# Hymba layer on one core: the last norm's tiles copied out of their banks, three tiles a chain at the end, and the SSD's out-projection put ahead of the LRU's in the last part

## The chip, the core and the metric

The kernel runs on one core of a Trainium2 chip. The time is device microseconds of one launch. The kernel before has a median of 3129.86 us over three runs (3123.33 to 3131.66); its profiled execution took 3120.88 us.

In the text PE is TensorE's matmul, PEld its weight load, DVE is VectorE, ACT is ScalarE, POOL is GpSimd, and SP is SyncE, which issues almost all DMAs. "Banks" are the eight PSUM tiles of 128 x 512 fp32 that matmuls write to. All times are in microseconds from the start of the profiled span.

## What is computed

One layer of a hybrid decoder, in fp32, for 2048 prompt tokens and 32 sample tokens (8 sequences of 4), with a width of 1024 and a feed-forward width of 4096. Cut to what matters here:

```python
h = rmsnorm(x, g_mix)
proj = h @ w_in
# group A: conv, RG-LRU, gelu gate, group norm  -> y_lru (1024 columns)
# group B: conv, Mamba-2 SSD in chunks, silu gate, two group norms -> y_ssd (1024)
x = x + concatenate([y_lru, y_ssd], axis=-1) @ w_out
m = rmsnorm(x, g_mlp)
x = x + square(relu(m @ w_up)) @ w_down
y = rmsnorm(x, g_final)
```

Outputs are `y` for prompt and sample tokens, and the states that both groups carry on.

## The kernel before

**Layout and precision.** Activations lie transposed: 128 channels on the partitions, tokens along the row. An fp32 product is three fp32r matmuls of a high and a low half of each operand (`mm3`, lines 232 to 234). The halves of a weight come from `load_w`: a DMA into `raw` (line 217), an ACT copy to `wh` (219) and a DVE subtraction to `wl` (221).

**The mix phase** runs over three parts of 768, 672 and 640 tokens, each in two blocks of tokens (the last part: 384 and 256). A part is projected in, goes through eight pairs of SSD heads and eight LRU heads, and is projected out by `proj_add` (427 to 445). The SSD heads form two norm groups. The first group's out-projection runs in the middle of the heads, the second's at the end of the part beside the LRU's. For an output tile `o` of 128 channels and a block, `proj_add` lets PE fill a bank, and DVE multiplies it by the norm's row factors (444) and adds it to the residual `X2[o]` (445). For the second SSD group an output has 4 chunks of 128 inputs in 2 blocks, so 24 matmuls and two pairs of these DVE operations; one `load_w` serves two outputs. Line by line in the order of the program, at the end of each part:

- outputs 0 to 5 of the second SSD group; between them, by `hook`, the LRU's eight gated results are split into halves (488) and their norm is summed;
- all eight outputs of the LRU;
- outputs 6 and 7 of the second SSD group;
- squares of `X2` on ACT, added up on DVE (455), for the next norm: in the last part those of outputs 0 to 5 before the SSD's last two outputs, those of 6 and 7 after. `carried_out` writes the carried states out by way of `st` copies.

`residual_out` then closes the part by block: token sums by PE (466, bank `nx`), a reciprocal root on DVE (`rsqrt`, 246 to 252, ten small operations however many columns), its spreading to rows (294 and 296), eight multiplications (1296), and for each the stores to `mn_d` (1298) and `x2_d` (1299) in DRAM.

**Jobs.** Beside this, 64 jobs of six stages turn the MLP's weights into seven combined blocks in DRAM (`up_d`, `dn_d`): a load, four DVE additions, an ACT copy and two DVE subtractions (1133), two stores. `tick`, called from the heads and from `proj_add`, issues one stage whenever `clock[1]` has come up by one; a last `tick(999)` issues what is left.

**The MLP** runs over three blocks of columns (`MLP`: twice 348, 346 and 346). It multiplies 2 x 2 blocks of operands by seven products in place of eight. `front` loads the normed residual from `mn_d` (856), forms the seven operands and splits them into halves (834 on ACT, 835 on DVE). `up` (seven `product`s of 12 matmuls, 827) and `down` (four times seven) then alternate, eight times each pair. Weights come from DRAM into six buffers `mw` (818 for up, 956 for down). `down` loads the residual back into its `x2` tiles (963) in a column block's first round, and adds the products to it (946).

**The final norm** (`final`, 990 to 1025) of a column block is cut into six tiles of up to 128 tokens. A tile is a `step`: four transposes by PE into a bank for each of two halves of the channels (1006); ACT squares the bank into a buffer `yt` and sums along the row (1008); DVE adds the two sums (1011, 1012), takes the reciprocal root, and multiplies both banks by it and the gain into the same `yt` (1016); SP stores both (1022). There are three `yt` buffers. The steps of column blocks one and two are the `fill` of the next block: each is issued behind product 0, 2, 4 or 6 of the next block's first two `up`s (`FILL`), in two banks of a pool of their own (`fx`). The steps of the last block run at the very end, in the MLP's six banks.

**What sets the order.** A scheduler lays out each engine's instructions, with the order of the program as priority, and every engine runs its own in that order. SP too works in order: a DMA that waits for its data or its buffer holds up all those behind it. Pools give their buffers round robin, so an instruction waits until the buffer's last user is done.

Of the kernel before, what the change touches and what calls it, by code (L numbers as in the profile page):

```python
# [8 lines left out]
F32 = mybir.dt.float32  # L9
# [29 lines left out]
TP, TL, TO, TX = 0.9, 1.35, 1.0, 1.0  # L39

# [7 lines left out]
def hymba_step(ctx: ExitStack, tc: tile.TileContext,  # L48
# [754 lines left out]
    def mlp(residual):  # L803
# [5 lines left out]
        room["w"], room["nx"] = (tl, 6), psf  # L809
        def bank():  # L810
            return ps8.tile([128, 512], F32, tag="mb", name="mb")
# [4 lines left out]
        def weights(src, op, m):  # L816
            w = mp.tile([128, 2, 512], F32R, tag="mw", name="mw", bufs=6)
            nc.sync.dma_start(w[:, :, :m].bitcast(F32), src[:, op])
            return w
# [167 lines left out]
        def final(c0, n, x2, end=False):  # L987
# [11 lines left out]
            def step(o, m):  # L999
                ss = sf.tile([128, 8], F32, tag="ssq", name="ssq")  # L1000
                s2 = sf.tile([128, 2], F32, tag="s2", name="s2")
                yts, pss = [], []
                for hf in range(2):
                    ps = bank() if end else psf.tile([128, 512], F32, tag="nx", name="fx")
                    for k in range(4):
                        T.transpose(ps[:m, 128 * k:128 * k + 128], x2[4 * hf + k][:, o:o + m], ident)
                    yt = mq.tile([128, 512], F32, tag="yt", name="yt", bufs=3)
                    S.activation(yt[:m], ps[:m], AF.Square, accum_out=s2[:m, hf:hf + 1])  # L1008
                    yts.append(yt)
                    pss.append(ps)  # L1010
                V.tensor_add(ss[:m, 0:1], s2[:m, 0:1], s2[:m, 1:2])
                V.tensor_scalar(ss[:m, :1], ss[:m, :1], 1.0 / D, EPS, op0=ALU.mult, op1=ALU.add)
                rs = sf.tile([128, 8], F32, tag="rs", name="rs")
                rsqrt(rs[:m], ss[:m], 1, sf)
                for hf in range(2):
                    V.scalar_tensor_tensor(out=yts[hf][:m], in0=pss[hf][:m], scalar=rs[:m, 0:1],  # L1016
                                           in1=gfb[:m, 512 * hf:512 * hf + 512], op0=ALU.mult, op1=ALU.mult)

                    for a, e, ap, r in ((0, s0, y_p, 0), (s0, s1, y_s, -s0), (s1, NTOK, y_p, -NS)):
                        lo, hi = max(a, c0 + o), min(e, c0 + o + m)  # L1020
                        if lo < hi:
                            nc.sync.dma_start(dap(ap, (lo + r) * D + 512 * hf, [[D, hi - lo], [1, 512]]),
                                              yts[hf][lo - c0 - o:hi - c0 - o])

            return [lambda a=a: step(*a) for a in steps]

        mh, steps = front(*MLP[0])
# [80 lines left out]
    clock = [0, 0.0]  # L1108
# [38 lines left out]
    def tick(w):  # L1147

        n = len(stages)
        clock[1] += w  # L1150
        while clock[1] >= 1 and clock[0] < n * len(jobs):
            clock[1] -= 1
            j, st = divmod(clock[0], n)
            stages[st](j)
            clock[0] += 1
# [33 lines left out]
    for P in parts:  # L1189
        dt_front(P)  # L1190
# [86 lines left out]
        proj_add(P, w_out, 12, n1, bc1, range(6), {o: (lambda o=o: hook(o)) for o in range(6)})  # L1277
# [23 lines left out]
        proj_add(P, w_out, 0, nl, bcl, hooks={5: lambda: next(xn, None)})  # L1301
        next(xn, None)
        if P.last:
            carried_out(P)
            sums(range(6))
        proj_add(P, w_out, 12, n1, bc1, range(6, 8))
        for _ in xn:
            pass
        sums(range(6, 8) if P.last else range(8))
        if not P.last:  # L1310
# [42 lines left out]
```

## Time and profile before

| What | Value |
|---|---|
| Median of three runs | 3129.86 us (3123.33 to 3131.66) |
| The profiled execution | 3120.88 us, of which 3119.1 us are its span |
| TensorE's mean granted clock | 0.963 of full speed |
| Mix phase, to the last matmul of the out-projection | from 0 to 1692.7 us |
| First to last matmul of the MLP | from 1727.9 to 3080.3 us |
| From there to the end | 38.8 us |

In a row of a window table stand the stretch, its length, and for each engine its busy time and, in brackets, its instructions; then the clock that TensorE was granted (1.00 is full), the share of time in which the 16 DMA engines were busy, and what they moved. In a row of a timeline stand the start, the duration, the engine, the line, the operation, out<-in, the shape and the count of like instructions run together; in square brackets how long the engine had been idle ahead of it and whose signal it was put down to. SPq is SP's queue: the time for which it was at issuing DMAs.

### The profile page before, as it was taken

What the parts mean: (1) busy time and instruction counts of PE and PEld (TensorE: products, weight loads), DVE (VectorE), ACT (ScalarE), POOL (GpSimd) and SP (SyncE); (2) the same over time, 40 slices, a digit from 0 to 9 for tenths busy, and PEclk for the clock granted to TensorE, in tenths of its full rate; (3) what the DMA queues carried; (4) which work ended last, traced back from release to release, by engine and by line L of the source; (5) the groups of instructions that cost most, each with busy time, mean ns of one, the idle gap of its engine ahead of it and who ended that gap; (6) DMA issues with size and microseconds to landing.
All of it is one profiled execution on the core that took longest, in us unless ns stands there. A gap on an engine that the chain in (4) does not pass through costs nothing.

```text
span 3119.1 us, 49521 instructions
## 1 busy us (share of the span) xinstructions
PE 2896.6 (93%) x18150; PEld 2797.3 (90%) x18150; DVE 2183.2 (70%) x4463; ACT 1380.8 (44%) x2556; POOL 164.5 (5%) x270
## 2 busy tenths in 40 slices
PE   7999998999999897999987899999899999899996
PEld 6999897888989796998977899999799998899995
DVE  6888788788877878887896655557554547554546
ACT  5554785445348834535862332324332324323222
POOL 0000120010002200000210000000000000000000
PEclk9999998999999998999988899999999999999997
DMA  5555556766665677565666988888888888888884
GB/s 175 157 189 158 179 176 196 241 198 202 195 186 173 198 233 240 157 202 171 193 195 205 329 266 283 274 274 281 269 271 283 267 283 279 273 273 276 270 277 145
DMA packets 534482, 709.00 MB, mean 227 GB/s; under 512 B 44421, under 2 KB 414265, under 8 KB 534240
## 3 DMA queue, kind: packets, MB, share of 16 engines
q1 hardware_dynamic: 534016, 705.56, 71.0%
q8 instruction: 144, 2.36, 0.3%
q0 software_dynamic: 224, 0.27, 0.1%
q14 instruction: 98, 0.80, 0.1%
HBM read 541.43 MB, written 164.27 MB: 226 GB/s over the span
## 4 chain that ended last, share of the span: by engine, by line
PE 40%; DVE 4%; DMA 3%; ACT 1%; issue 1%; SPq 1%; DVEq 0%; ACTq 0%
PE mb L827 38%; DMA out_dram<-yt 1%; DMA mb<-mn_d 0%; DMA mw<-dn 0%; DMA dn<-jt 0%; DVE yt L1016 0%; SPq L1115 0%; PE mm L234 0%; PE mm L233 0%; PE mm L232 0%; DVE ahl L835 0%; ACT yt L1008 0%; ACT mhh L834 0%; DMA x<-x_d 0%; DVE jt L1133 0%
## 5 line engine op out<-in xcount | busy, mean ns | idle before, releaser
L232 PE MATMUL mm<-xh,wh 128*128 128x384 f32 (+3 forms) x2160 | 715.1, 332 | 32.7 <-ACT xe L398 14.2
L234 PE MATMUL mm<-xh,wl 128*128 128x384 f32 (+3 forms) x2160 | 706.5, 328 | 3.8 <-DVE wl L221 3.7
L233 PE MATMUL mm<-xl,wh 128*128 128x384 f32 (+3 forms) x2160 | 706.9, 328 | 0.1
L827 PE MATMUL mb<-ahh,mw 128*128 128x346 f32 (+1 forms) x2688 | 656.5, 324 | 20.8 <-DVE nt L249 8.7
L827 PE MATMUL mb<-mhh,mw 128*128 128x346 f32 (+1 forms) x2688 | 651.8, 322 | 19.3 <-ACT mhh L834 18.7
L827 PEld LDWEIGHTS mb<-ahh,mw 128*128 128x128 f32 x2688 | 473.0, 190 | 28.2 <-DVE nt L249 9.5
L827 PEld LDWEIGHTS mb<-mhh,mw 128*128 128x128 f32 x2688 | 474.9, 190 | 20.5 <-ACT mhh L834 19.6
L232 PEld LDWEIGHTS mm<-xh,wh 128*128 128x128 f32 (+1 forms) x2160 | 410.6, 190 | 49.8 <-ACT xe L398 17.5
L827 PE MATMUL mb<-mhl,mw 128*128 128x346 f32 (+1 forms) x1344 | 437.1, 325 | 0.0
L827 PE MATMUL mb<-ahl,mw 128*128 128x346 f32 (+1 forms) x1344 | 435.1, 324 | 0.3
L234 PEld LDWEIGHTS mm<-xh,wl 128*128 128x128 f32 (+1 forms) x2160 | 409.2, 190 | 12.5 <-DVE wl L221 6.0
L233 PEld LDWEIGHTS mm<-xl,wh 128*128 128x128 f32 (+1 forms) x2160 | 410.5, 190 | 3.9 <-issue 1.0
L946 DVE TENSOR_TENSOR x<-x,mb 128x346 f32<-128x346 f32 (+1 forms) x480 | 244.2, 514 | 147.2 <-PE mb L827 143.8
L219 ACT ACTIVATE wh<-raw 128x1024 fp32r<-128x1024 f32 (+1 forms) x159 | 165.5, 1042 | 254.6 <-PE mm L233 204.5
L827 PEld LDWEIGHTS mb<-ahl,mw 128*128 128x128 f32 x1344 | 255.0, 190 | 1.2 <-DVE ahl L835 1.0
L827 PEld LDWEIGHTS mb<-mhl,mw 128*128 128x128 f32 x1344 | 254.8, 190 | 0.0
L905 ACT ACTIVATE p<-mb 128x346 f32<-128x346 f32 (+1 forms) x48 | 21.9, 455 | 474.2 <-PE mb L827 474.2
L221 DVE TENSOR_TENSOR wl<-raw,wh 128x1024 fp32r<-128x1024 f32 (+1 forms) x159 | 190.9, 1201 | 21.5 <-ACT wh L219 18.9
L411 DVE SCALAR_TENSOR_TENSOR u<-xe,prm,u 128x768 f32<-128x768 f32 (+2 forms) x180 | 170.0, 945 | 17.6 <-ACT u L409 15.4
L232 PE MATMUL mm<-nh,wh 128*128 128x384 f32 (+2 forms) x384 | 130.8, 341 | 29.5 <-DVE x L445 26.5
L932 ACT ACTIVATE c<-c 128x346 f32<-128x346 f32 (+1 forms) x144 | 71.2, 494 | 192.8 <-DVE c L918 115.4
L1130 ACT ACTIVATE jh<-jt 128x1792 fp32r<-128x1792 f32 x64 | 108.6, 1697 | 105.2 <-DVE jt L1126 89.6
(303 smaller groups left out, 4240.7 us busy)
## 6 DMA issues: line engine op xcount, KB each, us to landing
mw<-up SPq DMA_DIRECT2D x336, 512.0 KB
mw<-dn SPq DMA_DIRECT2D x288, 512.0 KB
raw<-in_w_in_dram SPq DMA_DIRECT2D x108, 512.0 KB
up<-jh SPq DMA_DIRECT2D x32, 896.0 KB
up<-jt SPq DMA_DIRECT2D x32, 896.0 KB
dn<-jh SPq DMA_DIRECT2D x32, 896.0 KB
dn<-jt SPq DMA_DIRECT2D x32, 896.0 KB
raw<-in_w_out_dram SPq DMA_DIRECT2D x48, 512.0 KB
```

The lines of the kernel that those rows point to most:

```text
L219: S.activation(h, raw, AF.Copy)
L221: V.tensor_tensor(out=lo, in0=raw, in1=h.bitcast(F32), op=ALU.subtract)
L232: T.matmul(ps[:m, :n], h[:, k, :m], xh[:, c0:c0 + n], start=k == 0, stop=False)
L233: T.matmul(ps[:m, :n], h[:, k, :m], xl[:, c0:c0 + n], start=False, stop=False)
L234: T.matmul(ps[:m, :n], lo[:, k, :m], xh[:, c0:c0 + n], start=False, stop=k == nk - 1)
L411: V.scalar_tensor_tensor(out=u[:, :W], in0=xe[:, k:k + W], scalar=pc(wn, k * nt + j), in1=u[:, :W], op0=ALU.mult, op1=ALU.add)
L827: T.matmul(ps[:, :n], w[:, wi, c], x[:, :n], start=start and k == 0 and i == 0, stop=k == nk - 1 and i == 2, skip_group_check=not start)
L905: S.activation(p1[:, :n], x[:, :n], AF.Copy)
L932: S.activation(c[:, :n], c[:, :n], AF.Relu)
L946: V.tensor_tensor(out=c, in0=c, in1=ps[:, :n], op=op)
L1130: S.activation(h, jt[j], AF.Copy)
```

## The change

Four edits.

1. **The final norm.** `step` takes a list of tiles. Inside the MLP (`end` false) it is still one tile, but ACT now copies the bank into `yt` behind its square (line 1020 of the new kernel), and DVE multiplies `yt` in place of the bank, so the bank's last reader is the copy. At the end (`end` true) a step takes three tiles, with one reciprocal root of three columns, and DVE reads the banks as before. `yt` has six buffers in place of three.
2. **The order of the out-projection in the last part.** All eight outputs of the second SSD group come ahead of the LRU's. The squares of output `o - 1` are called for ahead of the LRU's output `o`, and those of output 7 at the end, behind `carried_out`.
3. **The first five up-weights** are requested (`ahead`) before `front` asks for its rows.
4. **The clock of the jobs** runs 5% faster in the last part (`TF`).

```diff
+TF = (1.0, 1.0, 1.05)
...
+        ahead = []
...
         def weights(src, op, m):
+            if src is up_d[0] and ahead:
+                return ahead.pop(0)
...
-            def step(o, m):
+            def step(tiles):
+                w = len(tiles)
                 ss = sf.tile([128, 8], F32, tag="ssq", name="ssq")
-                s2 = sf.tile([128, 2], F32, tag="s2", name="s2")
-                yts, pss = [], []
-                for hf in range(2):
-                    ps = bank() if end else psf.tile([128, 512], F32, tag="nx", name="fx")
-                    for k in range(4):
-                        T.transpose(ps[:m, 128 * k:128 * k + 128], x2[4 * hf + k][:, o:o + m], ident)
-                    yt = mq.tile([128, 512], F32, tag="yt", name="yt", bufs=3)
-                    S.activation(yt[:m], ps[:m], AF.Square, accum_out=s2[:m, hf:hf + 1])
...
+                if any(m < 128 for _, m in tiles):
+                    V.memset(ss, 1.0)
+                for i, (o, m) in enumerate(tiles):
+                    s2 = sf.tile([128, 2], F32, tag="s2", name="s2")
+                    for hf in range(2):
+                        ps = bank() if end else psf.tile([128, 512], F32, tag="nx", name="fx")
+                        for k in range(4):
+                            T.transpose(ps[:m, 128 * k:128 * k + 128], x2[4 * hf + k][:, o:o + m], ident)
+                        yt = mq.tile([128, 512], F32, tag="yt", name="yt", bufs=6)
+                        S.activation(yt[:m], ps[:m], AF.Square, accum_out=s2[:m, hf:hf + 1])
+                        if not end:
+                            S.activation(yt[:m], ps[:m], AF.Copy)
+                        rows_.append((i, o, m, hf, yt, ps if end else yt))
+                    V.tensor_add(ss[:m, i:i + 1], s2[:m, 0:1], s2[:m, 1:2])
...
-                rsqrt(rs[:m], ss[:m], 1, sf)
-                for hf in range(2):
-                    V.scalar_tensor_tensor(out=yts[hf][:m], in0=pss[hf][:m], scalar=rs[:m, 0:1],
+                rsqrt(rs, ss, w, sf)
+                for i, o, m, hf, yt, src in rows_:
+                    V.scalar_tensor_tensor(out=yt[:m], in0=src[:m], scalar=rs[:m, i:i + 1],
...
-            return [lambda a=a: step(*a) for a in steps]
+            k = 3 if end else 1
+            return [lambda a=steps[i:i + k]: step(a) for i in range(0, len(steps), k)]
+        ahead.extend([weights(up_d[0], op, 512) for op in range(5)])
         mh, steps = front(*MLP[0])
...
-        clock[1] += w
+        clock[1] += w * TF[clock[2]]
...
-        proj_add(P, w_out, 12, n1, bc1, range(6), {o: (lambda o=o: hook(o)) for o in range(6)})
+        first_outs = 8 if P.last else 6
+        proj_add(P, w_out, 12, n1, bc1, range(first_outs), {o: (lambda o=o: hook(o)) for o in range(6)})
...
-        proj_add(P, w_out, 0, nl, bcl, hooks={5: lambda: next(xn, None)})
+        hooks = {o: (lambda o=o: sums([o - 1])) for o in range(1, 8)} if P.last else {5: lambda: next(xn, None)}
+        proj_add(P, w_out, 0, nl, bcl, hooks=hooks)
         next(xn, None)
         if P.last:
             carried_out(P)
-            sums(range(6))
-        proj_add(P, w_out, 12, n1, bc1, range(6, 8))
...
-        sums(range(6, 8) if P.last else range(8))
+            sums([7])
```

Three places show what this moves. The numbers at a row's end (x7) count like instructions in a row.

First, ACT in the first `up` of the second column block, where the final norm of the first column block is filled in (`mhh` and `ahh` are high halves, `fx` the fill's bank, `p` and `c` the MLP's own results). Before:

```order
L834 ACTIVATE mhh<-mb 128x346 x7
L1008 ACTIVATE yt,s_22650<-fx 128x512
L834 ACTIVATE mhh<-mb 128x346
L1008 ACTIVATE yt,s_22650<-fx 128x512
L913 ACTIVATE p_22751<-mb 128x346
L932 ACTIVATE c_22767<-c_22767 128x346
L922 ACTIVATE c_22819<-mb 128x346
L934 ACTIVATE c_22767<-c_22767 128x346
L934 ACTIVATE c_22819<-c_22819 128x346
L834 ACTIVATE ahh<-c_22819 128x346
L1008 ACTIVATE yt,s_22717<-fx 128x512
```

The same place after the change:

```order
L839 ACTIVATE mhh<-mb 128x346 x7
L1018 ACTIVATE yt,s_22650<-fx 128x512
L839 ACTIVATE mhh<-mb 128x346
L1020 ACTIVATE yt<-fx 128x512
L1018 ACTIVATE yt,s_22650<-fx 128x512
L1018 ACTIVATE yt,s_22719<-fx 128x512
L1020 ACTIVATE yt<-fx 128x512 x2
L918 ACTIVATE p_22755<-mb 128x346
L1018 ACTIVATE yt,s_22719<-fx 128x512
L927 ACTIVATE c_22825<-mb 128x346
L1020 ACTIVATE yt<-fx 128x512
L1018 ACTIVATE yt,s_22789<-fx 128x512
```

Before, the second tile's first square stood behind six operations of the first `up`; now it stands straight behind the first tile's second square, each square has its copy, and the third tile begins where the second began.

Second, SP where the mix phase hands over to the MLP (stores of `mn` to `mn_d`, loads of `front` into `mb`, weights into `mw`, the final gain into `gfb`). Before:

```order
L1298 DMA mn_d<-mn 128x384 x8
L1298 DMA mn_d<-mn 128x256 x7
L856 DMA mb<-mn_d 128x348 x12
L1298 DMA mn_d<-mn 128x256
L818 DMA mw<-up_142 128x1024 x2
L1040 DMA gfb<-in_g_final_dram 128x1024
L818 DMA mw<-up_142 128x1024
L856 DMA mb<-mn_d 128x348 x4
L818 DMA mw<-up_142 128x1024 x4
```

And after:

```order
L1313 DMA mn_d<-mn 128x384 x8
L1313 DMA mn_d<-mn 128x256 x7
L823 DMA mw<-up_142 128x1024 x5
L861 DMA mb<-mn_d 128x348 x12
L1313 DMA mn_d<-mn 128x256
L823 DMA mw<-up_142 128x1024 x2
L1053 DMA gfb<-in_g_final_dram 128x1024
L968 DMA x_18243<-x_d 128x696
L861 DMA mb<-mn_d 128x348 x4
```

The five weights have moved from behind the twelve rows and the last store to ahead of both, but still stand behind the first fifteen stores.

Third, DVE at the end of the last part's out-projection (`mm` is the bank, `x` the residual, `acc` the sum of squares, `st` the carried states). Before:

```order
L445 TENSOR_TENSOR x_14078<-x_14078,mm 128x256
L444 TENSOR_TENSOR mm<-mm,bc 128x384
L444 TENSOR_TENSOR mm<-mm,bc 128x256
L445 TENSOR_TENSOR x_14080<-x_14080,mm 128x384
L445 TENSOR_TENSOR x_14080<-x_14080,mm 128x256
L455 TENSOR_TENSOR acc<-acc,sq 128x384
L455 TENSOR_TENSOR acc<-acc,sq 128x256
L455 TENSOR_TENSOR acc<-acc,sq 128x384
L455 TENSOR_TENSOR acc<-acc,sq 128x256
L471 TENSOR_SCALAR ssq<-nx 128x3
```

And after:

```order
L445 TENSOR_TENSOR mm<-mm,bc 128x384
L446 TENSOR_TENSOR x_14089<-x_14089,mm 128x384
L445 TENSOR_TENSOR mm<-mm,bc 128x256
L1081 COPY st<-ax 3x512
L446 TENSOR_TENSOR x_14089<-x_14089,mm 128x256
L1095 COPY st<-ax 8x128
L1102 COPY st<-ax 128x512 x2
L456 TENSOR_TENSOR acc<-acc,sq 128x384
L456 TENSOR_TENSOR acc<-acc,sq 128x256
L472 TENSOR_SCALAR ssq<-nx 128x3
```

Two output tiles' sums stood between the last addition to the residual and the norm; now it is one, and the copies of the carried states stand there too.

More of the change, by code (lines that the diff above doesn't have):

```diff
@@ L997, in final @@
                 o += m
-            def step(o, m):
+            def step(tiles):
+                w = len(tiles)
                 ss = sf.tile([128, 8], F32, tag="ssq", name="ssq")
-                s2 = sf.tile([128, 2], F32, tag="s2", name="s2")
-                yts, pss = [], []
-                for hf in range(2):
-                    ps = bank() if end else psf.tile([128, 512], F32, tag="nx", name="fx")
-                    for k in range(4):
-                        T.transpose(ps[:m, 128 * k:128 * k + 128], x2[4 * hf + k][:, o:o + m], ident)
-                    yt = mq.tile([128, 512], F32, tag="yt", name="yt", bufs=3)
[L1008 to L1012, printed above, removed]
+                if any(m < 128 for _, m in tiles):
+                    V.memset(ss, 1.0)
+                rows_ = []
+                for i, (o, m) in enumerate(tiles):
[10 more added lines that the diff above has]
+                    V.tensor_add(ss[:m, i:i + 1], s2[:m, 0:1], s2[:m, 1:2])
+                V.tensor_scalar(ss[:, :w], ss[:, :w], 1.0 / D, EPS, op0=ALU.mult, op1=ALU.add)
@@ L1022, in step @@
                             nc.sync.dma_start(dap(ap, (lo + r) * D + 512 * hf, [[D, hi - lo], [1, 512]]),
-                                              yts[hf][lo - c0 - o:hi - c0 - o])
-            return [lambda a=a: step(*a) for a in steps]
+                                              yt[lo - c0 - o:hi - c0 - o])
+            k = 3 if end else 1
+            return [lambda a=steps[i:i + k]: step(a) for i in range(0, len(steps), k)]
+        ahead.extend([weights(up_d[0], op, 512) for op in range(5)])
         mh, steps = front(*MLP[0])
@@ L1107, in hymba_step @@
     jt, jh = {}, {}
-    clock = [0, 0.0]
+    clock = [0, 0.0, 0]
     def job_load(j):
@@ L1189, in hymba_step @@
     for P in parts:
+        clock[2] = P.i
         dt_front(P)
@@ L1304, in hymba_step @@
             carried_out(P)
-            sums(range(6))
-        proj_add(P, w_out, 12, n1, bc1, range(6, 8))
-        for _ in xn:
-            pass
-        sums(range(6, 8) if P.last else range(8))
-        if not P.last:
+            sums([7])
+        else:
+            proj_add(P, w_out, 12, n1, bc1, range(6, 8))
+            for _ in xn:
+                pass
+            sums(range(8))
             carried_out(P)
```

## Prediction

> **What bounds the kernel now.** I read the page first.
>
> ```profile
> span 3119.1 us, 49521 instructions
> PE 2896.6 (93%) x18150; PEld 2797.3 (90%) x18150; DVE 2183.2 (70%) x4463; ACT 1380.8 (44%) x2556; POOL 164.5 (5%) x270
> ```
>
> PE is busy for 93% of the span, and the change takes no matmul away. So it can only win PE's idle time (3119.1 - 2896.6 = 222.5 us) and time at a low clock. Where those lie near the edits, windows by stage tell:
>
> ```profile
> 1600.00:1626.00 26.00, 17.53 (x84) 15.14 (x85) 24.40 (x55) 13.90 (x24) 0.30 (x1) 0.74 0.65 208
> 1692.70:1728.00 35.30, 3.72 (x16) 3.24 (x16) 24.87 (x72) 7.54 (x18) 0.00 (x0) 0.57 0.62 210
> 1717.00:1728.00 11.00, 0.11 (x1) 0.14 (x1) 8.17 (x19) 5.53 (x13) 0.00 (x0) 0.50 0.93 307
> 1780.00:2130.00 350.00, 350.00 (x2195) 349.34 (x2194) 184.33 (x385) 100.19 (x226) 0.00 (x0) 1.00 0.84 276
> 2180.00:2232.00 52.00, 38.56 (x230) 35.85 (x229) 35.12 (x118) 20.35 (x53) 0.00 (x0) 0.90 0.76 241
> 2225.00:2230.00 5.00, 4.55 (x16) 4.56 (x17) 3.77 (x11) 0.46 (x1) 0.00 (x0) 0.50 0.75 268
> 2650.00:2690.00 40.00, 29.73 (x170) 27.27 (x169) 28.04 (x94) 13.57 (x36) 0.00 (x0) 0.87 0.76 240
> 3080.00:3119.10 39.10, 8.19 (x49) 6.42 (x47) 20.99 (x87) 8.02 (x24) 0.00 (x0) 0.59 0.20 73
> ```
>
> Within an MLP block PE has no idle time at all, at full clock, a matmul each 350.00 / 2195 = 0.159 us. The idle time lies at the seams: 31.6 us at the hand-over to the MLP, 13.4 and 10.3 us where one column block follows another, 30.9 us at the end, and 8.5 us in 1600 to 1626, where DVE is full. Who holds up the final norm, the view of its tile `yt` says:
>
> ```profile
>   PE fx L1006: 37.3, 14
>   DMA out_dram<-yt: 29.0, 12
> ```
>
> ACT's squares waited 29.0 us for stores out of `yt` and 37.3 us for transposes, which in turn wait for banks.
>
> **The end: -14 us (-10 to -16).** The timeline of the last 39 us:
>
> ```profile
> 3082.25 0.58 ACT L1008 ACTIVATE yt<-mb 128x512 f32<-128x512 f32 x1
> 3087.54 0.60 ACT L1008 ACTIVATE yt<-mb 128x512 f32<-128x512 f32 x1 [4.62 <-DMA out_dram<-yt]
> 3099.49 0.60 ACT L1008 ACTIVATE yt<-mb 128x512 f32<-128x512 f32 x1 [4.68 <-PE mb L1006]
> 3100.16 0.60 ACT L1008 ACTIVATE yt<-mb 128x512 f32<-128x512 f32 x1
> ...
> 3106.17 0.16 DVE L1011 TENSOR_TENSOR ssq<-s 128x1 f32<-128x1 f32 x1 [2.17 <-ACT yt L1008]
> 3108.55 1.41 DVE L1016 SCALAR_TENSOR_TENSOR yt<-mb,rs,gfb 128x512 f32<-128x512 f32 x2
> 3114.74 1.41 DVE L1016 SCALAR_TENSOR_TENSOR yt<-mb,rs,gfb 128x512 f32<-128x512 f32 x2
> 3085.45 31.06 SPq L1022 DMA_DIRECT2D out_dram<-yt  x14
> ```
>
> A tile costs 6.0 us (3087.54 to 3099.49 are two): with three `yt`, each waits for the store two buffers back. After the change the third square, at 3082.25, is followed by three more at a pitch of 0.67 us (3099.49 to 3100.16): done at 3085.0. The chain to the factors takes 3108.55 - 3106.17 = 2.4 us, whatever its columns: 3087.4. Six multiplications at 0.70: 3091.6. A buffer comes free 2.1 us after its store is issued (3085.45 to 3087.54), the first at 3087.4 + 0.7 + 2.1 = 3090.2; so squares of the second chain run from 3090.2 to 3094.6, factors stand at 3097.0, multiplications end at 3101.2. From the last multiplication's end (3116.15) to the span's end are 2.95 us: 3104.2, that is 15 us. I take 1 off since six 256 KB stores at that pace want 375 GB/s where 307 is the most in my rows. Nearest -10 if each chain's stores came at half that pace, -16 if the first buffers free a microsecond sooner.
>
> **The two seams between column blocks: -20 us (-8 to -27).** The first seam, with the price of a bank's copy from the groups by line:
>
> ```profile
> 2181.87 1.00 SPq L1022 DMA_DIRECT2D out_dram<-yt  x2
> 2188.48 0.60 ACT L1008 ACTIVATE yt<-fx 128x512 f32<-128x512 f32 x1 [2.70 <-DMA out_dram<-yt]
> 2194.71 0.63 PE L1006 MATMUL fx<-ident,x 128*128 128x128 f32 x4 [2.70 <-DVE yt L1016]
> 2219.13 1.44 PE L1006 MATMUL fx<-ident,x 128*56 128x128 f32 x8 [4.07 <-DVE yt L1016]
> 2225.45 0.66 PE L827 MATMUL mb<-ahh,mw 128*128 128x346 f32 x1 [4.88 <-DVE nt L249]
> 2220.18 2.33 SPq L963 DMA_DIRECT2D x<-x_d  x5
> 2224.87 0.52 DVE L946 TENSOR_TENSOR x<-x,mb 128x346 f32<-128x346 f32 x1 [1.54 <-DMA x<-x_d]
> ...
> L678 ACT ACTIVATE h0T<-ax 128x512 f32<-128x512 f32 x16 | 9.2, 594 | 2.8 <-PE ax L677 2.8
> ```
>
> Two things stand still. Transposes wait for a bank that DVE has yet to multiply (2.70, 4.07). And the last tile's transposes let `x2` be loaded only at 2220.18, so the first addition waits until 2224.87, banks stay full, and PE stands for 4.88 us; then it runs at half clock for about 4.6 us and loses 2.3 (row 2225:2230). All told 13.4 + 10.3 + 2 x 2.3 = 28.3 us gross. The copy frees a bank 0.6 us after the square, ahead of the factors; the new order has all six tiles' transposes in the first `up`, and so the loads of `x2` earlier. New costs: twelve copies by 0.59 (row L678, same shape) are 7 us of ACT per seam, which has 52 - 20 = 32 us free there; but ACT works in order, and a square that waits for its `yt` holds up the `mhh`, `p` and `c` behind it, and so PE. With six `yt` tile 4 waits for tile 1's store, and a store took up to 6.6 us here (2181.87 to 2188.48). In the new order some 45 matmuls stand between tile 1 and tile 4, 45 x 0.159 = 7 us, and tile 1 needs about 1.9 for its copies and second square, 2.4 + 1.4 for factors and multiplications, and 2.1 to 6.6 for the store: 8 to 12, and more when the store is queued behind a weight on SP. So tile 4 is 1 to 5 us late; nothing (0) if the scheduler's gaps stretch, some 10 if tiles 5 and 6 are late as well. I allow 4 us a seam: 28.3 - 8 = 20.
>
> The granted clock is 0.50 in 2225:2230 and the row's loss 2.3 us. The Trainium skill, "TensorE: Matmul & The Clock Gate", Part 1, says that half rate follows an idle window of about 3.4 us and ends after as much busy time, which would be an estimated 1.7 us a seam in place of 2.3, and 1.2 less in the sum.
>
> **The end of the mix phase: -6.5 us (0 to -12).** Timeline, and groups of DVE in 1609 to 1692.7:
>
> ```profile
> 1684.23 0.42 PE L232 MATMUL mm<-nh,wh 128*128 128x384 f32 x1
> 1692.38 0.28 PE L234 MATMUL mm<-nh,wl 128*128 128x256 f32 x1
> 1698.40 1.41 PE L466 MATMUL nx<-ones,acc 128*128 128x1 f32 x6 [5.74 <-DVE acc L455]
> ...
> L221 DVE TENSOR_TENSOR wl<-raw,wh 128x1024 fp32r<-128x1024 f32 x9 | 11.0, 1221 | 0.5
> L445 DVE TENSOR_TENSOR x<-x,mm 128x256 f32<-128x256 f32 (+1 forms) x22 | 10.6, 482 | 0.4
> L444 DVE TENSOR_TENSOR mm<-mm,bc 128x384 f32<-128x384 f32 (+1 forms) x21 | 10.5, 498 | 15.4 <-PE mm L234 15.4
> ```
>
> The SSD's last two outputs leave the end: 1692.66 - 1684.23 = 8.4 us. They go to 1600 to 1626, where PE has 8.5 us free but DVE 26.0 - 24.4 = 1.6. They bring DVE one `wl` (1.22) and four pairs (4 x 0.98): 5.1, of which 3.5 lengthen that stretch. Net -4.9. Behind the last matmul, 5.7 us pass until the sums; one output's squares go from there, the carried states' copies stay: I take 4.0, -1.7. If DVE gives nothing, 0; if the stretch swallows all, and with 1.7 more for its clock of 0.74, -12.
>
> **Five weights ahead of the rows: +1.5 us (-3 to +6).**
>
> ```profile
> 1714.94 6.16 SPq L856 DMA_DIRECT2D mb<-mn_d  x12
> 1721.80 0.81 SPq L818 DMA_DIRECT2D mw<-up  x2
> 1721.32 0.52 DVE L835 TENSOR_TENSOR mhl<-mb,mhh 128x348 fp32r<-128x348 f32 x1 [0.70 <-ACT mhh L834]
> 1727.89 0.63 PE L827 MATMUL mb<-mhh,mw 128*128 128x348 f32 x1 [17.23 <-ACT mhh L834]
> ```
>
> The first product's operands were ready at 1721.8 but it began at 1727.89: the wait is for the weight, issued at 1721.80 behind twelve rows, though the row names ACT. Now the weights go first. But 5 x 512 KB (2.62 MB) take 8.5 us at the 307 GB/s of 1717:1728, and the twelve rows (174 KB each, 2.1 MB) another 7.0; the second product needs all twelve. Before, it began 12 matmuls at half clock after the first: 1727.89 + 12 x 0.32 = 1731.7. Now the last row lands at about 1714.9 + 15.5 + 2.1 = 1732.5, plus a subtraction and halves at 0.5 each: 1733.5, 1.8 late. The first product can start early meanwhile, and the clock warm; +1.5. That the rows wait behind the weights is also what the Trainium skill says ("DMA: Bandwidth & Descriptors", Queues, rings and completion order: each DMA engine takes descriptors in ring order); if shared instead, the last row would land at the same time.
>
> **Denser jobs: +1 us (-3 to +5).**
>
> ```profile
> 1687.89 2.10 DVE L1133 TENSOR_TENSOR jt<-jt,jh 128x1024 fp32r<-128x1024 f32 x2
> ```
>
> The last job's operations, as this one of 2.1 us, go from the closing stretch into the heads, where DVE is the fuller engine; one or two such against it or for it bound it.
>
> **Sum.** -14 - 20 - 6.5 + 1.5 + 1 = -38 us. The profiled execution took 3120.88 (its span 3119.1), 9.0 below the median: 3082.9 for a like profile, 3129.86 - 38 = 3091.9 as a median. A measurement of this kernel can tell 0.3%, 9.4 us, from no change.
>
> **Rivals.**
> - *The ring takes the place of the banks* (0.17). Stores of `yt` stand in SP's order behind weights that wait for their buffers, tiles 4 to 6 each stall ACT, and so PE, for 4 us: 12 a seam in place of 4. The 29.0 us row speaks for it, the doubled ring against it. -38 + 16 = -22: 3108.
> - *DVE and the DMA queue hold the front* (0.13). The out-projection gains 0, the MLP starts 5 late, jobs cost 5: -14 - 20 + 10 = -24: 3106. For it: 24.4 of 26 us on DVE.
> - *Slower: weights starve behind `x2`* (0.03). SP now has loads of `x2` among the stores, ahead of the down weights; they wait for the last tile's transposes. Six weight buffers are six products of 1.9 us, so up to 11.5 us late costs nothing; beyond it PE idles, at half clock afterwards. Above 19 us more a seam the sum turns; at 22 it is 3136. Against it: with the bank freed early those transposes come sooner.
> - *The change does not do what it says* (0.05). The five weights still wait behind fifteen stores, the fill's order is held by its DVE chain as before, the mix phase by DVE: only the end gains, at its bound of -10, and +2.5 for weights and jobs stay: 3122.
>
> **Numbers.** The forecast has 0.62. The range, 3074 to 3112, holds it and the first two rivals; above it lies the rest, below it the good ends of seams and mix phase together. Faster by over 0.3% are the forecast and the first two rivals, 0.92; within it the last, 0.05; slower the third, 0.03.
>
> **What would show it.** At the end two bursts of six multiplications, and 25 us from last matmul to end (38.8 - 14). At the seams PE idle of 4 to 6 us each, ACT's waits on `out_dram<-yt` few; waits of several microseconds there are the first rival. In the mix phase no `nh` matmul behind the LRU's, and the last one some 5 us earlier. At the hand-over, the first product earlier against the last store, the second later. I am wrong if the seams keep over 10 us of idle each, or if the last part's heads grow.

## The result, and the profile after

The changed kernel takes 3083.16 us in the median of four runs (3080.22 to 3085.24) against 3126.6 us for the kernel before (four runs now, 3117.77 to 3131.66), a ratio of 0.986 (95% interval 0.9843 to 0.9877), 43.8 us less by the ratio. The forecast was 38 us less, and 3091.9 us from the median of 3129.86.

The page of the changed kernel, the same two lines as before:

```profile
span 3081.2 us, 49470 instructions
PE 2888.0 (94%) x18150; PEld 2789.5 (91%) x18150; DVE 2168.8 (70%) x4422; ACT 1390.9 (45%) x2580; POOL 171.1 (6%) x270
```

PE has as many instructions and nearly as much busy time; its idle time fell from 222.5 to 193.2 us. Windows over the two seams between column blocks and over the end:

```profile
2181.00:2233.00 52.00, 49.55 (x308) 48.11 (x307) 38.88 (x131) 24.83 (x64) 0.00 (x0) 0.97 0.94 332
2640.00:2682.00 42.00, 39.20 (x240) 37.24 (x240) 27.98 (x83) 14.60 (x36) 0.00 (x0) 1.00 0.94 336
3057.60:3081.20 23.60, 7.00 (x49) 6.28 (x46) 13.77 (x43) 7.63 (x24) 0.00 (x0) 0.72 0.32 120
```

PE's idle time in a seam went from 13.4 and 10.3 us to 2.5 and 2.8, and its clock hardly drops there. The DMA engines are busy for 0.94 of the time, at 332 and 336 GB/s. The view of the tile `yt`, what ACT waited for before its squares:

```profile
  PE fx L1016: 8.8, 4
  DMA out_dram<-yt: 3.7, 3
```

Waits for stores out of `yt` fell from 29.0 to 3.7 us, waits for the fill's transposes from 37.3 to 8.8. The 29.0 us are of two places, though. The same view of the fill's bank `fx`, which leaves out the end, has of the kernel before:

```profile
  DMA out_dram<-yt: 10.4, 8
```

So only 10.4 us of the waits for stores lay in the two fills; the other 18.6 lay at the end. In the fills the banks were the larger wait from the start. The end after the change, in the timeline:

```profile
3061.46 0.59 ACT L1018 ACTIVATE yt<-mb 128x512 f32<-128x512 f32 x1
3067.48 0.60 ACT L1018 ACTIVATE yt<-mb 128x512 f32<-128x512 f32 x1 [5.34 <-PE mb L1016]
...
3064.63 4.03 DVE L1027 SCALAR_TENSOR_TENSOR yt<-mb,rs,gfb 52x512 f32<-52x512 f32 x6
3074.19 4.04 DVE L1027 SCALAR_TENSOR_TENSOR yt<-mb,rs,gfb 128x512 f32<-128x512 f32 x6
3065.43 4.17 PE L1016 MATMUL mb<-ident,x 128*128 128x128 f32 x24 [4.99 <-DVE yt L1027]
3065.40 13.20 SPq L1033 DMA_DIRECT2D out_dram<-yt  x14
```

Six squares in a row, six multiplications in a row, twice: the two bursts that the prediction drew. (The first two rows are the last square of the first burst and the first of the second.) From the last product to the end it takes 23.6 us in place of 39.0. The hand-over to the MLP, in the timeline:

```profile
1697.95 0.80 PE L467 MATMUL nx<-ones,acc 128*128 128x1 f32 x6 [2.07 <-DVE acc L456]
1713.89 2.50 SPq L823 DMA_DIRECT2D mw<-up  x5
1716.44 8.95 SPq L861 DMA_DIRECT2D mb<-mn_d  x12
1733.48 1.74 SPq L861 DMA_DIRECT2D mb<-mn_d  x4
1723.66 1.91 ACT L839 ACTIVATE mhh<-mb 128x348 fp32r<-128x348 f32 x4 [13.64 <-DMA mb<-mn_d]
1724.21 0.66 PE L832 MATMUL mb<-mhh,mw 128*128 128x348 f32 x1 [14.61 <-ACT mhh L839]
```

The weights are asked for first, and the first product, which before waited for its weight, now waits for rows: the halves that it reads begin 25.7 us after the token sums.

**A table by stage.** Single executions differ by several us, so stages are measured inside one execution, between instructions that every kernel has at the same place of its work. All kernels make 7632 matmuls into `mm` and 8064 products' matmuls into `mb`. A part makes 2544 of the former. "First 5000" is the time to the 5001st, so the first two parts but for their last 88; "heads" is from there to the 6933rd, ahead of the last part's closing out-projection; "closing" from there to the first token sum (`nx`); "hand-over" from that to the 673rd product's matmul; a "seam" is 756 of these, from 84 ahead of the end of a column block (2605th to 3361st, 5293rd to 6049th); "end" from the last product to the span's end.

| Kernel | first 5000 | heads | closing | hand-over | seam 1 | seam 2 | end |
|---|---|---|---|---|---|---|---|
| before | 1150.4 | 404.9 | 143.0 | 140.0 | 146.3 | 143.7 | 39.0 |
| after | 1155.1 | 406.4 | 136.4 | 141.4 | 132.7 | 133.0 | 23.6 |

The profiled executions differ by 37.9 us in span, not 43.8: that of the kernel before (3120.88) was 5.7 us faster than its median, that of the changed kernel (3082.9) stood at its own. By stage, 4.7 us of this lie in the first 5000 matmuls, which both kernels make in one and the same order on TensorE. Over the 14 profiled executions of this study that stretch took from 1146.7 to 1158.4 us.

### The profile page after: what moved, and what is told of

Read it like the earlier page. It is cut to its first block, busy times and chain, and to the rows that moved or that the text cites. A ratio compares the mean times of both kernels' runs of the same rounds, so it can differ in the third digit from the quotient of the medians.

```text
span 3081.2 us, 49470 instructions
## 1 busy us (share of the span) xinstructions
PE 2888.0 (94%) x18150; PEld 2789.5 (91%) x18150; DVE 2168.8 (70%) x4422; ACT 1390.9 (45%) x2580; POOL 171.1 (6%) x270
## 4 chain that ended last, share of the span: by engine, by line
PE 47%; DVE 8%; DMA 5%; ACT 4%; issue 1%; SPq 1%; POOL 0%; DVEq 0%; ACTq 0%
PE mb L832 39%; PE mm L235 2%; PE mm L233 2%; PE mm L234 2%; DVE jt L1146 1%; SPq L1128 1%; DMA dn<-jt 1%; DMA up<-jt 1%; DMA mb<-mn_d 1%; DMA mw<-dn 1%; DMA m<-cum 1%; DVE u L412 1%; DVE yt L1027 1%; DVE th L794 0%; ACT jh L1143 0%
## 5 line engine op out<-in xcount | busy, mean ns | idle before, releaser
L233 PEld LDWEIGHTS mm<-xh,wh 128*128 128x128 f32 (+1 forms) x2160 | 409.0, 190 | 47.4 <-ACT xe L399 17.5
L234 PEld LDWEIGHTS mm<-xl,wh 128*128 128x128 f32 (+1 forms) x2160 | 409.0, 189 | 3.8 <-issue 1.0
L233 PE MATMUL mm<-nh,wh 128*128 128x384 f32 (+2 forms) x384 | 131.2, 342 | 30.8 <-DVE x L446 27.8
L1146 DVE TENSOR_TENSOR jt<-jt,jh 128x1024 fp32r<-128x1024 f32 (+1 forms) x128 | 137.9, 1094 | 25.0 <-ACT jh L1143 24.8
```

The source lines that it names most:

```text
L233: T.matmul(ps[:m, :n], h[:, k, :m], xh[:, c0:c0 + n], start=k == 0, stop=False)
L234: T.matmul(ps[:m, :n], h[:, k, :m], xl[:, c0:c0 + n], start=False, stop=False)
L1146: V.tensor_tensor(out=jt[j][:, a:b].bitcast(F32R), in0=jt[j][:, a:b], in1=jh[j][:, a:b].bitcast(F32), op=ALU.subtract)
```

## The experiments

The first eight have one time and one profile each, and are read by their stages (the table of all stands behind them). The last four have four times each, beside seven of the kernel before. Of the kernel before there is one profile, so each difference from it rests on one execution. Among the ten kernels that leave the changed seams as they are, seam 1 took 132.7 to 136.3 us and seam 2 133.0 to 133.6; the changed kernel's first profile has the shortest of both.

**no_copy.** The fill's banks are multiplied by DVE again, the rest of the change stays.

```diff
-                        if not end:
-                            S.activation(yt[:m], ps[:m], AF.Copy)
-                        rows_.append((i, o, m, hf, yt, ps if end else yt))
+                        rows_.append((i, o, m, hf, yt, ps))
```

> The changed kernel without ACT's copies in the fills: DVE multiplies the fill's banks themselves again, the six yt buffers and the chains of three at the end stay. Theory (the copy frees the bank ahead of the factors, and that is the seams' gain): the first and the second seam lose most of what they won, 13.6 and 10.8 us, so each is 9 to 14 us longer than in the changed kernel, PE's idle time there comes back with transposes waiting for DVE on yt, and the end stays at 23.6 us. About 3103 to 3108. Rival (the seams were held by stores out of three yt buffers, 29.0 us of waits, and six buffers alone cure them): both seams within 3 us of the changed kernel, about 3083.

It took 3099.47 us, with seams of 139.1 and 138.8 us and the end at 23.6. The seams gave back 6.5 and 5.9 us of 13.6 and 10.8: neither the theory's 9 to 14 nor the rival's under 3. The view of `yt` shows which wait came back:

```profile
  PE fx L1016: 29.3, 13
  DMA out_dram<-yt: 0.2, 1
```

With six buffers hardly a square waits for a store, but transposes again wait for banks.

**three_buffers.** The copies stay, `yt` has three buffers again, and so the end one tile a chain.

```diff
-                        yt = mq.tile([128, 512], F32, tag="yt", name="yt", bufs=6)
+                        yt = mq.tile([128, 512], F32, tag="yt", name="yt", bufs=3)
...
-            k = 3 if end else 1
+            k = 1
```

> The changed kernel with three yt buffers in place of six, and so one tile a chain at the end; the copies in the fills stay. Theory: banks come free early but each tile waits for the store two buffers back, so the seams give back part, 4 to 10 us each, with ACT waiting for stores out of yt; the end goes back to the 6.0 us cycle and 38 to 39 us. About 3106 to 3119. Rival (the copy alone makes the seams, the ring is of no account there): seams within 2 us of the changed kernel, only the end 15 us longer, about 3098.

It took 3104.05 us, with seams of 138.8 and 140.7 us and the end at 39.1. By its stages the theory held: 6.1 and 7.8 us came back at the seams. Its total, 3106 to 3119, was missed by 2 us. The view of `yt`:

```profile
  DMA out_dram<-yt: 37.5, 12
  PE fx L1016: 8.8, 4
```

And a square of the end in the timeline, which waits for a store again:

```profile
3070.70 0.60 ACT L1018 ACTIVATE yt<-mb 128x512 f32<-128x512 f32 x1 [4.68 <-DMA out_dram<-yt]
```

18.7 of the 37.5 us lie at the end, as before. In the fills, by the view of `fx`, they are these:

```profile
  DMA out_dram<-yt: 18.9, 8
```

Against 10.4 before: in the fills the stores now hold the squares and the banks hardly do. So copy and ring each free one of two resources: in seam 1 the copy alone wins 7.5 us and the ring alone 7.2, in seam 2 3.0 and 4.9; both together win 13.6 and 10.8.

**end_single.** Six buffers, but one tile a chain at the end.

```diff
-            k = 3 if end else 1
+            k = 1
```

> The changed kernel with one tile a chain at the end, six yt buffers kept. It tells whether the end's 15.4 us come from the shared chain of factors or from the longer ring. Theory as the prediction put it (chains of three make it): with six buffers squares no longer wait for stores, but DVE still runs six chains of 2.4 and six pairs of multiplications of 1.4 in turn, so the end takes about 2 + 6 x 3.8 + 3 = 28 us against 23.6, about 3087. Rival (the ring alone): the end within 1 us of 23.6, about 3083. A second rival (the shared chain alone): back to 38 us, 3098.

It took 3084.89 us, and the end 22.8 us. The first rival was right, and the theory that the shared chain makes the end fell. DVE's timeline shows why six single chains aren't slower:

```profile
3064.97 1.40 DVE L1027 SCALAR_TENSOR_TENSOR yt<-mb,rs,gfb 52x512 f32<-52x512 f32 x2
3066.36 0.14 DVE L1022 TENSOR_TENSOR ssq<-s 128x1 f32<-128x1 f32 x1
3067.63 1.41 DVE L1027 SCALAR_TENSOR_TENSOR yt<-mb,rs,gfb 128x512 f32<-128x512 f32 x2
3070.00 1.41 DVE L1027 SCALAR_TENSOR_TENSOR yt<-mb,rs,gfb 128x512 f32<-128x512 f32 x2
```

In these rows a tile's multiplications begin 2.66 and 2.37 us behind those of the tile before, not 3.8 (2.76 in the mean of all five steps, up to 3078.78), and the next tile's sum stands straight behind a multiplication: with squares ready early, the small operations of two tiles are laid into each other's gaps.

**old_order.** The last part's out-projection and sums as before, all else as changed.

```diff
-        first_outs = 8 if P.last else 6
+        first_outs = 6
...
-        if P.last:
-            carried_out(P)
-            sums([7])
-        else:
-            proj_add(P, w_out, 12, n1, bc1, range(6, 8))
+        if P.last:
+            carried_out(P)
+            sums(range(6))
+        proj_add(P, w_out, 12, n1, bc1, range(6, 8))
...
+        sums(range(6, 8) if P.last else range(8))
```

> The changed kernel with the last part's out-projection in the order of before: six outputs of the second SSD group, the LRU's eight, the SSD's last two, and the sums where they stood. Theory: from the last heads to the token sums of the closing norm it takes 143 us again in place of 136.4, 6.6 us more, and all behind it is shifted by that: about 3089. Rival (the 6.6 us are a difference between two executions, or come from the jobs' faster clock): that stretch stays within 2 us of 136.4, about 3083. Total times of single runs differ by several us, so the stretch decides.

It took 3082.3 us, and the closing 136.8 us, not 143. The theory fell: the gain of the closing stands without the new order.

**tf_one.** The new order, the jobs at their old clock.

```diff
-TF = (1.0, 1.0, 1.05)
+TF = (1.0, 1.0, 1.0)
```

> The changed kernel with the jobs of the last part at their old clock. Theory (the denser jobs cost the heads 1 to 1.5 us and win nothing at the end, where the copies of the carried states stand instead): the last part's heads (matmul 5000 to 6932 of the projections) take 404.9 us as before against 406.4, and the stretch to the token sums 136 to 138 against 136.4: total within 2 us of the changed kernel. Rival (the faster clock is what makes room at the end): the stretch to the token sums grows by 3 us or more.

It took 3081.31 us, and the closing 139.2 us, 2.7 more than with the faster clock: the rival's way, just short of its 3, and outside the theory's 136 to 138. The last job's subtractions on DVE and the first token sum, of `old_order` and then of `tf_one`:

```profile
1678.24 2.10 DVE L1146 TENSOR_TENSOR jt<-jt,jh 128x1024 fp32r<-128x1024 f32 x2 [0.41 <-ACT jh L1143]
1696.01 0.80 PE L467 MATMUL nx<-ones,acc 128*128 128x1 f32 x6 [3.62 <-DVE acc L456]
```

```profile
1687.04 2.09 DVE L1146 TENSOR_TENSOR jt<-jt,jh 128x1024 fp32r<-128x1024 f32 x2
1693.92 1.41 PE L467 MATMUL nx<-ones,acc 128*128 128x1 f32 x6 [1.89 <-DVE acc L456]
```

In the kernel before, that job stood at 1687.89, and the sum at 1698.40, 5.7 us behind the last matmul. With the denser clock it is out of the way some 18 us ahead of the sum, and the sum follows the last matmul after 3.6 us in the old order too. So the closing's 6.6 us are two overlapping gains: the order alone wins 3.9 (143.0 to 139.2), the clock alone 6.3 (143.0 to 136.8; 5.8 in `two_numbers` below, 137.3), both 6.6. The kernels with the clock at 1.05 lie between 135.9 and 137.3.

Where the clock's 6.3 lie, windows over the first part of the closing and over the rest show, of the kernel before and of `old_order`:

```profile
1555.40:1631.60 76.20, 63.47 (x368) 58.91 (x367) 66.71 (x115) 57.51 (x79) 13.22 (x11) 0.87 0.61 192
1631.60:1698.40 66.80, 60.15 (x415) 59.53 (x414) 47.36 (x87) 18.30 (x26) 0.00 (x0) 1.00 0.70 221
```

```profile
1559.20:1631.90 72.70, 61.01 (x367) 57.20 (x366) 62.71 (x107) 54.32 (x76) 11.23 (x11) 0.91 0.64 200
1631.90:1696.00 64.10, 60.49 (x416) 60.10 (x416) 47.90 (x89) 19.75 (x28) 0.00 (x0) 1.00 0.67 210
```

The stretch with the last heads and the splits is 3.5 us shorter, with 4.0 us less of DVE in it (8 instructions fewer), and the rest 2.7 shorter with as much DVE. That the first part shortens because DVE has less to do there is argued from these rows; no run took DVE work out of it by itself.

**no_ahead.** Nothing is asked for ahead of the rows.

```diff
-        ahead.extend([weights(up_d[0], op, 512) for op in range(5)])
```

> The changed kernel without the request of five weights ahead of the rows. Theory: the first product starts some 3 us later after the token sums (29.5 us as before, against 26.3), but the MLP's steady work is reached 1.4 us sooner: product 56 (672 matmuls in) at 140.0 us after the token sums against 141.4; in total 1 to 2 us faster, which a total time can't tell. Rival (the early weights are a gain, since the first products run earlier): product 56 is 2 to 3 us later than in the changed kernel.

It took 3075.18 us. The first product started 28.8 us after the sums (26.3 with the weights ahead), and the hand-over took 139.4 us against 141.4, as the theory had it. The last four rows, which wait for buffers that the halves free, were asked for at 1723.12, 29.8 us after the sums; in the changed kernel at 1733.48, 35.5 us after:

```profile
1709.27 5.72 SPq L861 DMA_DIRECT2D mb<-mn_d  x12
1715.66 1.02 SPq L823 DMA_DIRECT2D mw<-up  x2
1723.12 1.75 SPq L861 DMA_DIRECT2D mb<-mn_d  x4
```

**rows_first.** Four rows, the first weight, eight rows, four weights.

```diff
             def loads():
                 load(b11, 0, c0)
+                if c0 == 0:
+                    w0 = weights(up_d[0], 0, 512)
                 load(b12, 0, c0 + n)
                 load(b22, 512, c0 + n)
+                if c0 == 0:
+                    ahead.extend([w0] + [weights(up_d[0], op, 512) for op in range(1, 5)])
...
-        ahead.extend([weights(up_d[0], op, 512) for op in range(5)])
```

> The changed kernel with another order of the same requests: the first four rows, the first weight, the other eight rows, then four weights. Theory (the first product waits for its weight, the second for all twelve rows; each in the order of the queue): first product at about 23 us after the token sums (26.3 in the changed kernel, 29.5 before), product 56 at 135 to 138 us (141.4 and 140.0), so 4 to 6 us faster than the changed kernel. Rival (what limits the start is the sum of bytes, or ACT and DVE with the halves, whatever the order): product 56 within 1.5 us of 140 to 141.

It took 3072.96 us. The first product came at 23.3 us, as the theory said, but the hand-over took 140.4 us: the rival's row. The fifth product still began 2.5 us before that of `no_ahead` (36.9 us after the sums against 39.4). From there on PE waited for low halves from DVE:

```profile
1728.34 0.43 PE L832 MATMUL mb<-mhl,mw 128*128 128x348 f32 x1 [0.40 <-DVE mhl L840]
```

The seventh began 0.5 us behind that of `no_ahead` (43.7 against 43.2). An early first product wins nothing where later operands come no sooner. That its total is the lowest of the eight owes most to its first 5000 matmuls, which no edit touches: they took 1146.7 us, the least of all.

**act_queue.** The five weights from ACT's queue.

```diff
-        def weights(src, op, m):
+        def weights(src, op, m, eng=nc.sync):
...
-            nc.sync.dma_start(w[:, :, :m].bitcast(F32), src[:, op])
+            eng.dma_start(w[:, :, :m].bitcast(F32), src[:, op])
...
-        ahead.extend([weights(up_d[0], op, 512) for op in range(5)])
+        ahead.extend([weights(up_d[0], op, 512, nc.scalar) for op in range(5)])
```

> The changed kernel with the five weights requested from ACT's queue in place of SP's, so that they stand behind no store of the norm's rows. Theory (they are late because SP works in order behind fifteen stores): they are issued some 3 us earlier than 1713.9, behind ACT's last copy of the factors, and both weights and rows land earlier: product 56 at 137 to 140 us after the token sums in place of 141.4. Rival (the DMA engines' rate bounds the sum of both): product 56 within 1 us of 141.4; or later, if the weights' packets now share the engines with the rows and hold both up.

It took 3083.47 us, and the hand-over 144.2 us, the longest of all. ACT's timeline, and the line of its requests in the view of `mw` (shortest, median and longest in ns):

```profile
1708.93 12.19 ACTq L823 DMA_DIRECT2D mw<-up  x5
1721.16 1.64 ACT L839 ACTIVATE mhh<-mb 128x348 fp32r<-128x348 f32 x4 [12.16 <-DMA mw<-up]
L823 ACTq DMA_DIRECT2D mw<-up x5: 326/327/444, 1708.9 to 1720.8; - x5
```

The first request came 12.0 us after the sums, in place of 15.9 from SP, as the theory had it. But the five were spread over 12.19 us, where SP made them in 2.50, and the first halves stood behind them in ACT's order. ACT was not slow at asking: a request took it 0.33 to 0.44 us. Between them it waited for semaphores. The five use two in turn, so that the fourth (1718.79) and the fifth (1720.79) stood until the second and the third (1714.51 and 1714.87) had landed; the second had stood 5.2 us until an earlier transfer on its semaphore had landed (1714.43). So the question it was made for, whether SP's order or the DMA engines' rate holds the weights, stays open: the wait only changed its place.

**The four timed runs.** `two_numbers` is the kernel before with `bufs=6` for `yt` and the jobs' clock of 1.05, and nothing else:

```diff
+TF = (1.0, 1.0, 1.05)
...
-                    yt = mq.tile([128, 512], F32, tag="yt", name="yt", bufs=3)
+                    yt = mq.tile([128, 512], F32, tag="yt", name="yt", bufs=6)
...
-        clock[1] += w
+        clock[1] += w * TF[clock[2]]
...
     for P in parts:
+        clock[2] = P.i
```

> The kernel before with two numbers changed and nothing else: six yt buffers in place of three, and the jobs' clock 1.05 in the last part. The order of the out-projection, the requests at the hand-over, DVE's reading of the banks and one tile a chain stay as before. Theory from the runs so far (the ring alone makes the end and half of each seam; the jobs' clock alone makes the end of the mix phase): end 22.8 us (39.0 before), seams about 139.1 and 138.8 (146.3 and 143.7), from the last heads to the token sums 136.8 (143.0), hand-over as before: -16.1 - 7.2 - 4.9 - 6.3 = -34.5 us against before, about 0.989 of it. Rival (the changed order, chains and copies were needed for these): the end of the mix phase stays over 140 us, or the end over 30, and the gain is under 25 us.

It took 3092.93 us in the median against 3129.67 on the same chip, a ratio of 0.9889 (0.9872 to 0.9907): 34.7 us less, where the stages added up to 34.5. The two numbers make four fifths of the whole change.

`best` is the changed kernel without the weights ahead and with one tile a chain (the edits of `no_ahead` and `end_single` together):

```diff
-            k = 3 if end else 1
+            k = 1
...
-        ahead.extend([weights(up_d[0], op, 512) for op in range(5)])
```

> The changed kernel without the weights ahead and with one tile a chain at the end; copies, six buffers, new order and denser jobs stay. Theory: 2.0 us won at the hand-over (product 56 at 139.4 us after the token sums), 0.7 at the end (22.8 in place of 23.6), the rest as in the changed kernel: 2.7 us faster than that, which the two intervals can hardly part. Rival: the two edits disturb each other or the seams and nothing is won.

3079.08 us, 0.9841 (0.9825 to 0.9858).

`best_tf110` is the same with the clock at 1.10:

```diff
-TF = (1.0, 1.0, 1.05)
+TF = (1.0, 1.0, 1.1)
```

> The kernel without the weights ahead and with one tile a chain at the end, and the jobs' clock in the last part at 1.10. Theory (DVE's job work in the closing stretch is what the faster clock moves into the heads, where DVE is idle for some 23 us): the stretch from the last heads to the token sums falls from 136.4 to 133 to 135 us, with the heads (406 to 407 us over eight runs) no longer than 408. Rival (with the last job out of the very end nothing more is late there, and the heads pay for it): the stretch stays at 136 or more, or the heads grow by 2 us or more.

3077.72 us, 0.984 (0.9818 to 0.9863). The closing took 137.3 us: the rival's first half was right, a still faster clock wins nothing there. Its second half, longer heads, did not come (405.5). The 23 us for which the expectation has DVE idle in the heads do not fit the trace: in the heads of `best` (1156.2 to 1562.6) DVE was busy for 337.4 of 406.4 us.

`after_again` is the changed kernel:

> The changed kernel itself once more, timed beside the other three on one chip. Every theory expects 0.986 of the kernel before, within its interval, and stages as in its first profile: 23.6 us at the end, seams of 132.7 and 133.0, 136.4 to the token sums. It gives the spread of the parts that no edit touches.

3082.46 us, 0.9861 (0.9838 to 0.9883). All stages of the first profile repeated within 1 us but the first 5000 matmuls (1150.5) and the heads (403.5). `best` and `best_tf110` are the fastest by their medians, some 3 to 5 us below the changed kernel, but the intervals of the three overlap: by total time they are not told apart, by stages 2.8 us at the hand-over and 0.7 at the end are.

| Kernel | first 5000 | heads | closing | hand-over | seam 1 | seam 2 | end |
|---|---|---|---|---|---|---|---|
| no_copy | 1158.4 | 408.6 | 136.3 | 143.3 | 139.1 | 138.8 | 23.6 |
| three_buffers | 1149.7 | 405.6 | 136.3 | 141.8 | 138.8 | 140.7 | 39.1 |
| end_single | 1153.5 | 409.0 | 136.4 | 141.8 | 135.6 | 133.5 | 22.8 |
| old_order | 1153.6 | 405.6 | 136.8 | 142.5 | 133.7 | 133.5 | 23.6 |
| tf_one | 1149.0 | 405.7 | 139.2 | 142.0 | 136.3 | 133.6 | 23.6 |
| no_ahead | 1153.7 | 403.3 | 136.4 | 139.4 | 133.4 | 133.5 | 23.6 |
| rows_first | 1146.7 | 407.6 | 135.9 | 140.4 | 134.1 | 133.1 | 23.6 |
| act_queue | 1148.2 | 411.8 | 136.9 | 144.2 | 134.2 | 133.6 | 23.6 |
| two_numbers | 1152.4 | 411.6 | 137.3 | 139.1 | 138.9 | 139.4 | 23.1 |
| best | 1156.2 | 406.4 | 136.6 | 138.3 | 134.1 | 133.1 | 22.8 |
| best_tf110 | 1150.6 | 405.5 | 137.3 | 139.4 | 133.6 | 133.5 | 22.8 |
| after_again | 1150.5 | 403.5 | 136.1 | 141.8 | 133.6 | 133.1 | 23.6 |

## Why the prediction was right, step by step

**The sum was right and so were its largest terms.** 38 us less was forecast, 43.8 measured, and the forecast's 3091.9 lies 8.7 above the median of the changed kernel.

**The end: -14 forecast, -15.4 measured.** The steps of the working came out: the second burst of squares begins 2.08 us after the first store is asked for (3065.40 to 3067.48), the multiplications take 0.67 us each, and 2.97 us lie behind the last. But the row of that square names its transposes, and these had stood 4.99 us for a bank that DVE had yet to multiply. The prediction left the banks out of its sum for the end, and here they and the buffers come free almost together. Its cause was only half read: the 6.0 us cycle was rightly put down to three buffers, but the gain was then worked out by way of chains of three. `end_single` and `two_numbers` show that the six buffers alone bring it (22.8 and 23.1 us), `three_buffers` that without them all of it is gone (39.1). The shared chain of factors wins nothing.

**The seams: -20 forecast, -24.4 measured** (13.6 + 10.8). The mechanism was right; the stalls that would remain were put at 4 us a seam and came out at 2.5 and 2.8. The prediction gave the gain to the copy and saw the ring as a limit on it; the runs give each about half. The first rival (the ring takes the place of the banks) would have been right with three buffers: 18.9 us of waits for stores in the fills. The 29.0 us that the prediction gave as speaking for it were mostly of the end (18.6).

**The end of the mix phase: -6.5 forecast, -6.6 measured, and the step behind it was wrong.** The number came out right by luck, by two errors that cancel. Even its split did: the last matmul came 4.4 us earlier and the sums followed it 2.2 us sooner, where 4.9 and 1.7 were forecast, but `old_order` has 4.1 and 2.1 without the step that was to bring them. "The SSD's last two outputs leave the end" wins 3.9, not 6.5, when it stands alone. And the denser jobs, booked at +1 as work pushed into fuller heads, win 6.3 alone. The prediction had the row that says so, the last job's subtractions at 1687.89 in the closing stretch, and read it as a cost that moves elsewhere. The heads took 403.3 to 411.8 us over eleven executions with the clock at 1.05, mean 407.2, against 404.9 and 405.7 with the old clock: a price of 1 or 2 us there is neither shown nor excluded.

**The weights ahead: +1.5 forecast, +1.4 in the first pair, +2.8 over the runs.** With the weights ahead on SP the hand-over took 141.4 to 143.3 us in seven executions, mean 142.1; without any ahead 138.3 to 140.0 in five, mean 139.3. The sign holds, and the reason (weights ahead of the rows, put at 8.5 us) fits. The step that failed is its place: the second product was to be late, yet it came 30.9 us after the sums against 33.1 before. The first halves begin 25.7 us after the sums in place of 19.3 (1717.70 against 1698.40), and the last four rows are asked for after 35.5 in place of 30.8; of the kernel before:

```profile
1717.70 0.94 ACT L834 ACTIVATE mhh<-mb 128x348 fp32r<-128x348 f32 x2 [6.62 <-DMA mb<-mn_d]
1729.20 1.75 SPq L856 DMA_DIRECT2D mb<-mn_d  x4
```

The loss comes behind the second product: the fifth products of both kernels begin level (39.8 and 39.9 us after the sums), the sixth at 43.5 against 41.9, since PE stands within the fifth for a low half (0.41) and a weight (0.67). That the late halves and rows are what makes this wait is argued from these rows. The prediction's reading of the first product's wait, that the row names ACT but the weight was late, is borne out: with the weight early it starts 0.55 us behind the first of its halves.

On the rule of the Trainium skill ("DMA: Bandwidth & Descriptors", Queues, rings and completion order), by which descriptors are taken in ring order, the trace agrees as far as it goes: twelve rows asked for behind five weights were first used 25.7 us after the sums, in `rows_first`, where the first four rows stand ahead of all five weights, after 18.4. On the rule of the clock in the Trainium skill ("TensorE: Matmul & The Clock Gate", Part 1) no run here decides between 1.7 and 2.3 us a seam: in the changed kernel's seams, idle for 2.5 and 2.8 us in all, the granted clock stayed at 0.97 and 1.00.

**The rivals.** None of the four ruled. The second had DVE hold the mix phase; by the windows of `old_order` it did, but the change relieved it by its fourth edit, which that rival counted as a loss.

## What to carry to other kernels

When a stage turns in a fixed cycle and its waits name a store, count the buffers first: one number, three to six, made the whole gain of the end and, alone, about half of each seam's, and together with a second number four fifths of a four-part change. Work that has to be done anyway is not free where it stands: here background work at the end of a stage, just ahead of its closing chain, cost more than the same work some microseconds earlier. A view that adds up a wait over the whole kernel does not say where the wait lies; ask for it by stage. And a total that comes out as forecast does not confirm its terms; undo each part alone, and measure stages within one execution, since an identical first part here differed by up to 11.7 us between executions.

## What the runs showed of the hardware

A request for a 512 KB load took ACT 0.33 to 0.44 us, and SP made five in 2.50 us; the 12.19 us over which ACT's five were spread are waits for the semaphores of transfers, during which ACT's own work was held too. In the seams of the changed kernel the DMA engines moved 332 and 336 GB/s with a busy share of 0.94, more than the 307 GB/s that the prediction took as the most in its rows. The kernel before had a window with still more, among the MLP's first products, which the prediction did not read:

```profile
1740.30:1745.00 4.70, 4.70 (x31) 4.70 (x30) 3.71 (x9) 3.79 (x10) 0.00 (x0) 1.00 0.99 362
```
